# A decoder step on one core: each engine's instruction order taken from the scheduler's timeline simulation

## Chip, cores, metric

One core of one Trainium2 chip runs the whole program. The metric is device time in microseconds (us) of one launch, input and output transfers of the kernel's own queues included; lower is better.

## What is computed

One layer (DEPTH = 1) of a decoder for a prompt group of 1024 positions and a sample group of 8 sequences by 8 positions with 512 cached positions each. All in fp32; D_MODEL = 1024, D_FF = 2816.

```
xn = rmsnorm(x) ; z = xn @ w_in                     # 1024 -> 2820 columns, four head groups
y  = [ RG-LRU(z_A) | gated short conv(z_B) | forgetting attention(z_C) | differential attention(z_D) ]
x  = x + y @ w_out
x  = x + (silu(rmsnorm(x) @ w_gate) * (rmsnorm(x) @ w_up)) @ w_down
y_out = rmsnorm(x)                                  # plus the new K/V rows and states as outputs
rg_lru: r, i = sigmoid(...);  a = exp(-8 r softplus(-lam));  u = sqrt(1 - a*a) * i * x;  h = a*h + u
```

## The kernel before, in words

The weights come in fp32 and every product with them is made of three matmuls on split operands: a high part (`xTh`, `whi`) and the rest (`xTl`, `wlo`). `mm3` (L92) issues the three in a row: L94 high by high, L95 and L96 the two mixed ones. The split of a weight block is one ScalarE copy (L325) and one subtraction on VectorE or GpSimd (L326); blocks come from `WStream.load_to` (L310, L312) into a ring of three `raw` buffers on SyncE's queue.

The prompt is worked in two halves of 512 positions, the sample group beside the first. A list of small closures, `prog`, is the program's order: the norms and the input projection of half 0, then half 1; attention of half 0 mixed by cost (`merge`, L1252) into the projection of half 1; the output projection, mixed with the sample group's attention (L1421 transposes of cached keys, L1436 scores, L1509 values); attention of half 1 mixed into the first feed-forward blocks; then the feed-forward network, most of it as a seven-product Winograd form (L1743). `run` (L1270) calls the closures in order, which only traces instructions.

Attention is a chain for each pair of query blocks: scores on TensorE (L1057, L1061), maximum on VectorE (L1081 to L1097), exponential on ScalarE (L1099, and a scaling L1103), transposes on TensorE (L1141), their split on ScalarE and VectorE (L1145, L1146), values on TensorE (L1161), sum (L1173, L1178). The RG-LRU gates are two small matmuls for each chunk (L854) with sigmoids (L855), an exponential and a tanh (L860, L861) and a square root (L870) on ScalarE.

PSUM is eight banks: three `mm`, two `s`, two `t`, one `o`.

What the engines run is not the traced order. When the `with` block of the tile library's context closes, its scheduler plays the traced program through a simulated machine. Whenever an engine of that machine is free it gets an instruction whose inputs and buffers are ready there, the earliest in the traced order first; the order in which this happens is written out as that engine's order, which the chip then follows strictly. Only instructions passed through `keep` (`tc.keep_in_program_order`) stay in the traced order among each other. They are found in the head of the program (norm of the first half, its first projections) and at a few places behind it; nearly everything else is free.

## Time and profile before

| | |
|---|---|
| median of 3 runs | 1379.26 us (1373.75 to 1382.87) |
| the profiled execution | 1379.24 us, of which the span of its instructions is 1376.9 us |
| granted TensorE clock, mean | 0.991 |
| TensorE busy | 1345.7 us, 98% of the span |
| VectorE, ScalarE, GpSimd busy | 1060.9, 675.6, 126.7 us |

Busy time is the union of an engine's records. The granted clock is the share of 2.4 GHz that the throttle let through; 0.5 would be 1.2 GHz throughout. PEld is the weight load that goes before each matmul. A wait is idle time of an engine that ends when another engine, or a transfer, signals.

### The profile page before, as it was taken

The numbers are of one execution on the slowest core, as the hardware profiler recorded it, in microseconds if no ns is written. First come the engines' busy times: TensorE is split into PE (matmuls) and PEld (weight loads), VectorE is DVE, ScalarE is ACT, GpSimd is POOL, SyncE is SP. The second block draws the span as 40 slices with busy tenths as digits, with TensorE's granted clock in tenths as the row PEclk, the third lists the DMA queues.
The fourth block names the chain that finished last, engine by engine and source line by source line (L and its number), as shares of the span: only waits on it lengthen the run. The fifth ranks groups of instructions, "written<-read, shape, count | busy, mean of one in ns | idle before, by whom it ended". The sixth has DMA issues, their size and how long they took to land.

```text
span 1376.9 us, 23077 instructions
## 1 busy us (share of the span) xinstructions
PE 1345.7 (98%) x8477; PEld 1181.9 (86%) x8477; DVE 1060.9 (77%) x2699; ACT 675.6 (49%) x1326; POOL 126.7 (9%) x154
## 2 busy tenths in 40 slices
PE   9899998999999999999999999999999999999997
PEld 7799896878876688888888999997999999999996
DVE  6676377788556568899979988547998888888885
ACT  6575466756333258755544444324533444444454
POOL 3001012302243011000000000000200000000001
PEclk9999999999999999999999999999999999999999
DMA  8566438666994366444236433611624333333311
GB/s 260 175 194 205 132 125 266 205 201 222 343 333 142 108 216 217 139 138 123 77 115 196 125 92 93 191 47 62 197 63 123 93 92 92 93 92 93 93 47 69
DMA packets 202866, 202.65 MB, mean 147 GB/s; under 512 B 16529, under 2 KB 165549, under 8 KB 202626
## 3 DMA queue, kind: packets, MB, share of 16 engines
q1 hardware_dynamic: 189568, 168.60, 40.2%
q0 software_dynamic: 7328, 25.11, 5.0%
q10 hardware_dynamic: 5858, 7.47, 1.5%
q8 instruction: 67, 1.10, 0.3%
q14 instruction: 45, 0.37, 0.1%
HBM read 170.56 MB, written 32.29 MB: 147 GB/s over the span
## 4 chain that ended last, share of the span: by engine, by line
PE 81%; DVE 6%; ACT 6%; DMA 5%; issue 1%; SPq 0%; ACTq 0%; POOL 0%; DVEq 0%
PE pb_mm L94 11%; PE pb_mm L95 10%; PE pb_mm L96 10%; PE pb_mm L1743 8%; PE pb_s L1743 5%; PE pb_t L1743 5%; PE pb_t L94 3%; PE pb_t L95 2%; PE pb_t L96 2%; PE pb_o L1743 2%; PE pb_s L96 2%; PE pb_s L95 2%; PE pb_s L94 2%; PE pb_o L1161 2%; PE pb_t L1141 2%; DMA raw<-in_w_in_dram 2%
## 5 line engine op out<-in xcount | busy, mean ns | idle before, releaser
L325 ACT ACTIVATE whi<-raw 128x512 fp32r<-128x512 f32 (+1 forms) x409 | 251.8, 629 | 350.9 <-PE pb_mm L96 75.5
L326 DVE TENSOR_TENSOR wlo<-raw,whi 128x512 fp32r<-128x512 f32 (+1 forms) x405 | 275.8, 692 | 70.5 <-ACT whi L325 60.6
L94 PE MATMUL pb_mm<-xTh,whi 128*128 128x512 f32 (+2 forms) x536 | 192.3, 359 | 0.8 <-ACT whi L325 0.8
L95 PE MATMUL pb_mm<-xTl,whi 128*128 128x512 f32 (+2 forms) x536 | 191.1, 357 | 0.3 <-DVE xTl L452 0.3
L96 PE MATMUL pb_mm<-xTh,wlo 128*128 128x512 f32 (+2 forms) x536 | 190.6, 356 | 0.3 <-DVE wlo L326 0.3
L96 PEld LDWEIGHTS pb_mm<-xTh,wlo 128*128 128x128 f32 x536 | 101.0, 188 | 13.7 <-issue 1.6
L94 PEld LDWEIGHTS pb_mm<-xTh,whi 128*128 128x128 f32 x536 | 101.3, 189 | 12.7 <-ACT whi L325 1.1
L95 PEld LDWEIGHTS pb_mm<-xTl,whi 128*128 128x128 f32 x536 | 101.2, 189 | 10.8 <-DVE xTl L452 0.5
L94 PE MATMUL pb_mm<-whi,xTh 128*128 128x256 f32 (+1 forms) x312 | 91.1, 292 | 0.0
L1099 ACT ACTIVATE aP<-aP,anm 128x128 f32<-128x128 f32 (+7 forms) x96 | 74.0, 772 | 34.5 <-DVE anm L1097 32.2
L95 PE MATMUL pb_mm<-wlo,xTh 128*128 128x256 f32 (+1 forms) x312 | 88.3, 283 | 0.2 <-POOL wlo L326 0.2
L96 PE MATMUL pb_mm<-whi,xTl 128*128 128x256 f32 (+1 forms) x312 | 88.2, 283 | 0.0
L1829 DVE TENSOR_TENSOR acc<-acc,pb_mm 128x512 f32<-128x512 f32 (+1 forms) x95 | 64.4, 678 | 15.1 <-PE pb_mm L96 13.2
L94 PE MATMUL pb_mm<-whi,hTh 128*128 128x512 f32 (+1 forms) x179 | 70.7, 395 | 0.3 <-ACT hTh L1803 0.3
L96 PE MATMUL pb_mm<-whi,hTl 128*128 128x512 f32 (+1 forms) x179 | 70.6, 394 | 0.0
L95 PE MATMUL pb_mm<-wlo,hTh 128*128 128x512 f32 (+1 forms) x179 | 70.3, 393 | 0.0
L94 PEld LDWEIGHTS pb_mm<-whi,xTh 128*128 128x128 f32 x312 | 59.0, 189 | 5.0 <-issue 4.2
L95 PEld LDWEIGHTS pb_mm<-wlo,xTh 128*128 128x128 f32 x312 | 59.0, 189 | 0.8 <-POOL wlo L326 0.4
L96 PEld LDWEIGHTS pb_mm<-whi,xTl 128*128 128x128 f32 x312 | 58.9, 189 | 0.6 <-issue 0.4
L1743 PE MATMUL pb_mm<-xTh,whi 128*128 128x288 f32 (+1 forms) x184 | 53.7, 292 | 0.0
L1743 PE MATMUL pb_mm<-xTh,wlo 128*128 128x288 f32 (+1 forms) x184 | 53.6, 292 | 0.0
L1743 PE MATMUL pb_mm<-xTl,whi 128*128 128x288 f32 (+1 forms) x184 | 53.6, 292 | 0.0
(623 smaller groups left out, 3778.3 us busy)
## 6 DMA issues: line engine op xcount, KB each, us to landing
raw<-in_w_gate_dram SPq DMA_DIRECT2D x44, 512.0 KB
raw<-in_w_up_dram SPq DMA_DIRECT2D x44, 512.0 KB
raw<-in_w_down_dram SPq DMA_DIRECT2D x22, 1024.0 KB
raw<-in_w_in_dram SPq DMA_DIRECT2D x12, 1024.0 KB
raw<-in_w_in_dram SPq DMA_DIRECT2D x16, 512.0 KB
raw<-in_w_out_dram SPq DMA_DIRECT2D x8, 1024.0 KB
akt<-fkD SPq DMA_DIRECT2D x24, 256.0 KB
akt<-dkD SPq DMA_DIRECT2D x48, 128.0 KB
```

The lines of the kernel that those rows point to most:

```text
L94: kp(nc.tensor.matmul(out, lhsT=lh, rhs=rh, start=first, stop=False))
L95: kp(nc.tensor.matmul(out, lhsT=lh, rhs=rl, start=False, stop=False))
L96: kp(nc.tensor.matmul(out, lhsT=ll, rhs=rh, start=False, stop=last))
L325: i1 = nc.scalar.activation(hi, s, AF.Copy)
L326: i2 = (nc.gpsimd if pool else nc.vector).tensor_tensor(lo, s, hi.bitcast(F32), op=OP.subtract)
L1099: nc.scalar.activation(dst[:, :ln], dst[:, :ln], AF.Exp, bias=nmx, accum_out=sm)
L1141: nc.tensor.transpose(pt[:, o:o + 128], P[ti][:, kb * 128:(kb + 1) * 128], ident)
L1161: nc.tensor.matmul(po[:, q0:q0 + n], lhsT=v[:, kb, :], rhs=a[:, o:o + n], start=kb == 0 and i == 0, stop=kb >= nkb - 2 and i == 1, skip_gr ...
L1743: nc.tensor.matmul(pt, lhsT=w[:, k], rhs=x[:, k], start=first and k == 0 and i == 0, stop=k == 3 and i == 2, skip_group_check=True)
L1829: nc.vector.tensor_tensor(a, a, pt, op=OP.add)
```

## The change

One keyword is given to the tile library's context. With it the scheduler plays the program through the library's timeline simulation instead of its plain one; the traced program, the rule by which a free engine gets its next instruction, the pinned instructions, tiles and buffer counts stay the same. What can differ is the order on each engine and each queue, and with it the waits and the buffer that a tile gets.

```diff
-    with _tile.TileContext(nc) as tc:
+    with _tile.TileContext(nc, schedule_with_timeline_sim=True) as tc:
         hybrid_step(tc, I, C, O)
```

## Rows read from the trace of the kernel before

**Rows 1.** The page, part 1: busy time, share of the span, instructions.
```profile
PE 1345.7 (98%) x8477; PEld 1181.9 (86%) x8477; DVE 1060.9 (77%) x2699; ACT 675.6 (49%) x1326; POOL 126.7 (9%) x154
```
**Rows 2.** Windows by stage: busy time of each engine, clock, DMA share, GB/s.
```profile
0.00:200.00 200.00, 190.91 (x1270) 173.53 (x1271) 130.62 (x341) 119.52 (x221) 26.12 (x34) 0.99 0.57 178
200.00:350.00 150.00, 141.67 (x834) 119.89 (x833) 117.68 (x502) 94.28 (x229) 32.87 (x45) 0.99 0.71 232
350.00:500.00 150.00, 145.32 (x1051) 111.97 (x1051) 81.40 (x213) 46.13 (x91) 38.78 (x48) 0.95 0.65 218
500.00:575.00 75.00, 73.90 (x429) 61.75 (x428) 64.16 (x213) 59.93 (x108) 10.02 (x19) 1.00 0.67 213
575.00:700.00 125.00, 124.98 (x653) 103.49 (x652) 118.68 (x373) 73.24 (x138) 4.09 (x4) 1.00 0.36 107
700.00:975.00 275.00, 274.60 (x1729) 244.50 (x1728) 210.00 (x417) 113.05 (x211) 0.00 (x0) 1.00 0.40 121
975.00:1350.00 375.00, 375.00 (x2428) 350.82 (x2427) 323.13 (x603) 157.31 (x300) 10.05 (x3) 1.00 0.31 92
1350.00:1377.00 27.00, 19.35 (x96) 15.96 (x94) 15.23 (x43) 12.11 (x30) 4.80 (x2) 0.92 0.25 88
```
**Rows 3.** Windows of 25 us in which the granted clock is below 0.95.
```profile
50.00:75.00 25.00, 22.27 (x154) 20.94 (x154) 21.20 (x98) 12.64 (x28) 0.00 (x0) 0.93 0.64 192
275.00:300.00 25.00, 22.96 (x122) 18.50 (x120) 20.60 (x94) 14.53 (x39) 0.00 (x0) 0.93 0.59 175
425.00:450.00 25.00, 22.36 (x135) 14.63 (x135) 16.92 (x46) 7.78 (x15) 5.04 (x6) 0.81 0.26 88
450.00:475.00 25.00, 24.82 (x158) 15.50 (x154) 12.09 (x34) 5.88 (x12) 0.94 (x1) 0.91 0.33 106
```
**Rows 4.** Waits of PE: us in total, times, longest.
```profile
PE pb_t L967 <- DVE lgf L953: 3.1, 2, 2.7
PE pb_t L1141 <- ACT aP L1103: 2.2, 5, 0.6
PE pb_o L1161 <- DVE aAl L1146: 2.0, 1, 2.0
PE pb_s L1061 <- DMA akt<-dkD: 1.7, 1, 1.7
```
**Rows 5.** Timeline of PE around one of these waits (start, us, instruction).
```profile
281.07 0.40 PE L95 MATMUL pb_mm<-xTl,whi 128*128 128x512 f32 x1
283.14 0.33 PE L1061 MATMUL pb_s<-akt,aqt 128*128 128x128 f32 x1 [1.67 <-DMA akt<-dkD]
283.31 0.45 PE L96 MATMUL pb_mm<-xTh,wlo 128*128 128x512 f32 x1
```
**Rows 6.** Groups of ScalarE by line: table loads of the RG-LRU gates.
```profile
L855 ACT ACT_TABLE_LOAD x7 | 9.0, 1283 | 0.7 <-PE pb_t L854 0.5
L860 ACT ACT_TABLE_LOAD x4 | 5.1, 1283 | 0.1
L870 ACT ACT_TABLE_LOAD x4 | 5.1, 1283 | 0.1
```
**Rows 7.** Timeline of ScalarE around one table load.
```profile
83.20 0.19 ACT L430 ACTIVATION_READ_ACCUMULATOR nxs<-nxt 128x1 f32 x1
83.40 1.28 ACT L855 ACT_TABLE_LOAD   x1
84.70 0.89 ACT L855 ACTIVATE lr<-pb_t,colR 128x288 f32<-128x288 f32 x2
```
**Rows 8.** Waits of PEld for the gates' ScalarE work.
```profile
PEld pb_t L854 <- ACT lr L855: 1.0, 2, 0.7
```
**Rows 9.** Waits of SyncE's queue before weight loads.
```profile
SPq L310 <- DVE wlo L326: 172.5, 16, 17.4
SPq L312 <- DVE wlo L326: 137.8, 16, 16.8
```
**Rows 10.** The chain that ended last: its one long transfer after 575 us.
```profile
952.29 4.02 DMA raw<-in_w_gate_dram
```

## The prediction

> **What bounds the kernel now.** First the page's busy line [rows 1]: TensorE is busy in 1345.7 us of a span of 1376.9, so 31.2 us are all that any order can take from its idle time. The same instructions run after the change, in another sequence; TensorE's 8477 matmuls and their weight loads don't get fewer or shorter by being reordered. Then the windows by stage [rows 2], to see where the 31.2 us lie. The reader subtracts the first busy figure from the length of each stretch: 9.1 us in 0 to 200 (norms, projections, RG-LRU), 8.3 in 200 to 350 (attention of half 0), 4.7 in 350 to 500 (sample attention and output projection), 1.1 in 500 to 575 and 7.7 in the last 27 us; from 575 to 1350, more than half of the span, 0.4 us in 775. In that part no order can be better, only worse. Third, the granted clock, since a low clock makes TensorE busy for longer without idling [rows 3]: four windows of 25 us have 0.93, 0.93, 0.81 and 0.91. Time at the lower of the two levels (1.2 GHz) does half the work, so the loss in full-clock time is (0.07 + 0.07 + 0.19 + 0.09) x 25 = 10.5 us. Fourth, what ended TensorE's waits [rows 4]: single events of 0.5 to 3 us, each an instruction that stood first in TensorE's order while its input came late. The timeline at one of them shows what kind of thing it is [rows 5]: the source issues L94, L95 and L96 in a row, but the order has an attention score (L1061) between L95 and L96, and it waits 1.67 us for a key transfer while L96, which then runs within 0.2 us, was held behind it. So the scheduler does move instructions, and its simulated machine was wrong there about when the transfer lands. That is the one thing the change touches.
>
> **The change term by term**, against the profiled execution's own 1379.24 us (span 1376.9 and 2.3 around it; the median of the runs is 1379.26, and the runs spread over 9 us, so 1% is about what a measurement of this kernel can tell from no change).
>
> 1. *The work.* The same instructions, 0.
>
> 2. *Waits taken away.* A model that places inputs in time better would not put an instruction first whose input is late. The trace does not show the new order, so I bound it. Most: half of the idle time of 0 to 575 us, (9.1 + 8.3 + 4.7 + 1.1) / 2 = 11.6, and half of the clock's 10.5, 5.2; together 16.8. Least: 0. I take the two longest single waits of attention in the rows, 2.0 (L1161) and 1.7 (L1061) [rows 4], as gone: -3.7. I stay near the low end because the list is long and its entries short: the next of its kind, L1141, is 2.2 us in five pieces, and removing one usually shows the next instruction of the same chain as the late one.
>
> 3. *Waits added.* Every place where the new order puts an instruction earlier than its input is a new wait, and behind it on TensorE wait all the ready matmuls, as L96 does above. Least 0; most, the idle time of 0 to 575 once more, 23.2, and the clock's 10.5 once more, 33.7. I take three waits of the size of the key transfer's, 3 x 1.7 = +5.1, since such waits are of one kind with those that the present order has.
>
> 4. *Table loads on ScalarE.* ScalarE reloads its function table when its order goes from one kind of function to another: 7 + 4 + 4 = 15 loads of 1.283 us in the lines of the gates alone [rows 6], 19.2 us. Their number hangs on ScalarE's order. They cost TensorE little: its loader waits 1.0 us in two events for this work [rows 8], because projection matmuls fill the time and ScalarE is busy in 119.5 of the first 200 us [rows 2]. Bounds: -1.0 if the loads that show are gone, +19.2 if as many come on top and all stand in TensorE's way. I take 0, the nearer row being the 1.0. The Trainium skill, ScalarE: Activation LUTs, section "What ACT_TABLE_LOAD costs", gives 1283 ns for the load and about 1380 ns for a drain, some 2.66 us for each switch. The row has the load, and no drain with it: the instruction before ends at 83.39, the load runs from 83.40 to 84.68 and the next activation starts at 84.70 [rows 7]. By the page 15 further loads would be an estimated 40 us of ScalarE.
>
> 5. *VectorE from 575 to 700* is busy in 118.7 of 125 us [rows 2], with TensorE never idle. If its order splits weights ahead of emptying PSUM banks, TensorE has no bank to write. What covers this is the set of eight banks, and 6.3 us of slack in the stretch. I take 0; if the cover is gone the cost is at most the slack's size again, +6.3, as VectorE's work itself fits.
>
> 6. *The transfer queues.* SyncE's queue waits for its weight buffers, 172.5 us in 16 events at one line and 137.8 in 16 at the other, always for VectorE's split [rows 9]: loads are issued when a buffer falls free, and TensorE does not wait for them. Late in the program one such load stands on the chain that ended last, 4.0 us, with TensorE hardly idle [rows 10]. An attention load moved ahead of a weight load in this queue delays that by its own transfer only. 0, bounds -0.4 (the idle time of 575 to 1350) and +4.0. GpSimd's queue is busy in 126.7 us in all [rows 1]; 0.
>
> 7. *The end.* The last 27 us have 7.7 without a matmul: the final norm and the store after the last products. These depend on each other and can't be reordered: 0, +-1.
>
> Sum: 1379.24 - 3.7 + 5.1 = 1380.6 us. That is, no change that a measurement can tell.
>
> **The rivals.**
>
> *Better order pays (faster).* For it: idle time and low clock in the first 575 us are of the order's making, as the 1.67 us wait shows. Against: entries are short and a chain's next member waits too; and the largest loss, 0.81 at 425 to 450, is where the sample group's chain has few matmuls left to fill with (135 matmuls in 25 us, against 162 in the mean of 975 to 1350 [rows 2, 3]). With both halves of term 2: 1379.24 - 16.8 = 1362.4.
>
> *Attention stages starve TensorE (slower).* One mechanism: in 200 to 500, chains of attention and sample work are slotted between dense matmuls, and the new order puts them a little too early. Each event is 0.5 to 2 us, with the clock falling after a group of them, as in the windows of 275, 425 and 450. Price: the idle time of 200 to 575 a second time, 8.3 + 4.7 + 1.1 = 14.1, and the clock's loss there, (0.07 + 0.19 + 0.09) x 25 = 8.75, together 22.9: 1402. It decides once the added waits are over about 14 us, eight of the 1.7 us kind. For it: TensorE has no more than 1 to 2% idle to give, and every misjudged input costs directly. Against: waiting instructions need their inputs late on the chip, and the present order, also made on a model, keeps such events to some 14 us.
>
> *Table switches (slower).* ScalarE takes sigmoids, exponentials and square roots of the gates as they come ready, and doubles its 15 loads; TensorE's transposes and gate matmuls in 75 to 190 us wait for banks behind them: 1379.24 + 19.2 = 1398.4. It decides when TensorE waits for more than half of the new loads. Against it: the covering matmuls of this stretch, and ScalarE's 80 us of idle time in the first 200. The Trainium skill, ScalarE: Activation LUTs, section "Table sets: the hidden batching unit", has the rule beside it: batch activations by set, not by function. By that rule an order that follows readiness alone would pay here; the trace so far shows the loads and nearly no wait for them.
>
> *Nothing to see.* The two simulated machines agree wherever it matters, and what moves stays within slack: 1379.2.
>
> **How the numbers follow.** Forecast (mixed, within 1%) 0.45; nothing to see 0.06; better order pays 0.19; attention starves 0.20; table switches 0.10. Faster by over 1% (under 1365.5): 0.19. Within 1%: 0.51. Slower by over 1% (over 1393): 0.30. For the range I reach from just below the faster rival, 1360, to above the slower ones, 1406, which leaves out the outer parts of these three, some 0.2 in all; the bound of term 3, 1413, is in that rest. The forecast's own range is 1366 to 1393.
>
> **What would show it.** The number of instructions per engine stays (table loads apart). From 575 to 1350 the windows show TensorE idle under 2 us. The idle time of 0 to 575 stays between 15 and 35 us, with other lines among its enders. The loads of L855, L860 and L870 are 10 to 20. If a window after 575 has TensorE idle by several us, the reason is a bank or a weight buffer that VectorE's new order frees late, and terms 5 and 6 were wrong; if the clock falls in more windows than four, term 3 was too small; if idle time before 575 is below 12 us, term 2 was.

## The result and the profile after

The changed kernel takes 1445.66 us (median of four runs, 1444.07 to 1449.28) against 1377.99 us (four runs): a ratio of 1.050 with a 95% interval of 1.0475 to 1.0526. The forecast was no change, 1380.6, with a range up to 1406; it was wrong by 65 us.

The profiled execution took 1444.07 us with a span of 1442.3. The page's busy line (busy time, share of the span, instructions), which answers to [rows 1]:

```profile
PE 1372.7 (95%) x8477; PEld 1207.1 (84%) x8477; DVE 1067.7 (74%) x2699; ACT 674.1 (47%) x1326; POOL 121.4 (8%) x154
```

The counts are those of before. TensorE idles for 1442.3 - 1372.7 = 69.6 us, 38.4 more than before, and is busy for 27.0 us more with the same matmuls; 38.4 + 27.0 = 65.4 is the whole difference of the spans. The windows by stage, with the columns of [rows 2], say where:

```profile
0.00:200.00 200.00, 188.87 (x1235) 172.46 (x1236) 121.06 (x320) 116.48 (x219) 23.68 (x32) 0.97 0.56 176
200.00:350.00 150.00, 146.63 (x879) 128.28 (x877) 128.77 (x506) 95.23 (x233) 35.07 (x49) 1.00 0.75 246
350.00:500.00 150.00, 131.09 (x938) 97.67 (x936) 73.63 (x199) 39.74 (x79) 34.80 (x42) 0.92 0.56 186
500.00:575.00 75.00, 74.47 (x373) 60.96 (x374) 47.62 (x132) 36.52 (x66) 6.30 (x13) 1.00 0.53 163
575.00:700.00 125.00, 125.00 (x664) 106.23 (x663) 100.46 (x278) 74.00 (x132) 7.50 (x11) 1.00 0.49 146
700.00:975.00 275.00, 252.56 (x1572) 224.40 (x1572) 212.75 (x518) 115.95 (x218) 1.82 (x2) 0.93 0.37 112
975.00:1350.00 375.00, 371.76 (x2324) 341.86 (x2323) 316.11 (x612) 157.36 (x301) 7.54 (x3) 1.00 0.32 94
```

The idle time has gone down by 5.0 us in 200 to 350, the first half's attention, and up by 14.2 in 350 to 500 and by 22.0 in 700 to 975, a stretch that had 0.4 before. The windows of 25 us in which most is lost, with the granted clock in the third column from the end (answering to [rows 3]):

```profile
25.00:50.00 25.00, 21.27 (x156) 20.64 (x155) 10.16 (x28) 10.61 (x24) 7.73 (x12) 0.84 0.68 213
350.00:375.00 25.00, 18.27 (x112) 16.87 (x111) 10.10 (x35) 6.21 (x16) 3.84 (x4) 0.71 0.81 287
375.00:400.00 25.00, 21.06 (x134) 18.28 (x132) 7.47 (x15) 3.95 (x7) 9.10 (x11) 0.81 0.87 281
725.00:750.00 25.00, 25.00 (x124) 20.79 (x123) 23.45 (x58) 11.65 (x23) 0.00 (x0) 1.00 0.19 53
750.00:775.00 25.00, 18.78 (x81) 13.20 (x79) 21.59 (x93) 13.34 (x26) 1.82 (x2) 0.70 0.13 43
800.00:825.00 25.00, 17.75 (x89) 14.76 (x89) 19.53 (x45) 10.50 (x17) 0.00 (x0) 0.86 0.61 182
825.00:850.00 25.00, 20.97 (x119) 20.07 (x120) 17.74 (x35) 10.47 (x21) 0.00 (x0) 0.73 0.65 194
```

From 575 to 750 TensorE is full at 1.00, and in the next window it is not. What ran out there is seen when TensorE's matmuls are counted by line, those of the attention (L1057, L1061, L1141, L1161, L1205, L1221; 848 in all) and the dense ones (projections and feed-forward), as started by a time:

| us | before: dense / attention | after: dense / attention |
|---|---|---|
| 500 | 2251 / 264 | 2168 / 264 |
| 600 | 2479 / 589 | 2508 / 409 |
| 700 | 2780 / 814 | 2819 / 625 |
| 750 | 2977 / 848 | 2996 / 690 |
| 800 | 3277 / 848 | 3032 / 844 |

Before, the second attention ends near 713 us, with dense matmuls left for 56 us until the Winograd blocks begin (first L1743 at 769). After, TensorE is ahead with the dense work by 700 and at 750 has used it up, while 158 attention matmuls remain; in the next 50 us only 36 dense ones run. Then the Winograd blocks start without their weights prepared: of the 22.4 us that TensorE idles from 700 to 975, 11.1 lie in 750 to 800, beside the end of the attention, and 11.3 in 800 to 850, most of them in front of Winograd products (L1743). The one long piece of the chain that ended last in this stretch is a load of them (start, us), which answers to [rows 10]:

```profile
825.84 8.09 DMA raw<-in_w_up_dram
```

Why the attention falls behind is seen in TensorE's timeline. ScalarE has finished the first high part for the value products at 576.62 (the two L1145 together run from 576.02 to 577.11):

```profile
576.74 0.40 PE L95 MATMUL pb_mm<-wlo,hTh 128*128 128x512 f32 x1
576.98 0.39 PE L96 MATMUL pb_mm<-whi,hTl 128*128 128x512 f32 x1
...
579.77 0.39 PE L96 MATMUL pb_mm<-whi,hTl 128*128 128x512 f32 x1
580.00 0.28 PE L1161 MATMUL pb_o<-aAh,avt 128*128 128x256 f32 x1
```

Fourteen dense matmuls go ahead of the value product that was ready at 576.62. This is no wait, TensorE is busy throughout, and so no list of waits shows it. Over the 160 split parts that the value products read, 3.9 matmuls of other work start, in the mean, between the end of a split and the first product that reads it in the kernel before, and 11.9 in the changed one. Between the first score and the last value product of the second attention TensorE's order has 527 dense matmuls before, in runs of 3.5 in the mean (1 of 150 runs has nine or more), and 726 after, in runs of 8.1 (36 of 90).

The list of TensorE's waits, with the columns of [rows 4], has new entries, all short; the last three are of the stretch from 750 to 850:

```profile
PE pb_mm L94 <- ACT xTh L565: 6.2, 2, 3.7
PE pb_t L1141 <- DVE aP L1113: 4.0, 3, 2.3
PE pb_t L1421 <- DMA spgk<-in_cache_fox_k_dram,idx: 3.9, 1, 3.9
PE pb_t L1221 <- DVE arb L1216: 3.9, 2, 3.6
PE pb_s L1743 <- ACT whi L325: 3.1, 1, 3.1
PE pb_s L1061 <- DVE aP L1084: 2.3, 3, 1.4
PE pb_t L1743 <- DVE wtl L1669: 2.1, 2, 2.0
```

ScalarE's table loads by line, which answer to [rows 6], are the same; with the smaller groups there are 24 in either profile:

```profile
L855 ACT ACT_TABLE_LOAD x7 | 9.0, 1283 | 2.6 <-PE pb_t L854 2.5
L860 ACT ACT_TABLE_LOAD x4 | 5.1, 1283 | 0.1
L870 ACT ACT_TABLE_LOAD x4 | 5.1, 1283 | 0.1
```

And SyncE's queue stands twice as long before the weight loads of L310, and less before those of L312 [rows 9]:

```profile
SPq L310 <- DVE wlo L326: 349.2, 28, 18.9
SPq L312 <- DVE wlo L326: 109.5, 18, 17.7
```

### The profile page after: what moved, and what is told of

Same layout as the page of the kernel before. It is cut to its first block, busy times and chain, and to the rows that moved or that the text cites. A ratio compares the mean times of both kernels' runs of the same rounds, so it can differ in the third digit from the quotient of the medians.

```text
span 1442.3 us, 23079 instructions
## 1 busy us (share of the span) xinstructions
PE 1372.7 (95%) x8477; PEld 1207.1 (84%) x8477; DVE 1067.7 (74%) x2699; ACT 674.1 (47%) x1326; POOL 121.4 (8%) x154
## 4 chain that ended last, share of the span: by engine, by line
PE 85%; DVE 6%; DMA 4%; ACT 3%; issue 1%; SPq 1%; ACTq 0%; POOL 0%; DVEq 0%
PE pb_mm L94 12%; PE pb_mm L95 12%; PE pb_mm L96 12%; PE pb_mm L1743 7%; PE pb_t L1743 5%; PE pb_s L1743 5%; PE pb_t L94 3%; PE pb_t L95 3%; PE pb_t L96 3%; PE pb_o L1161 2%; PE pb_s L95 2%; PE pb_s L94 2%; PE pb_s L96 2%; PE pb_t L1141 2%; PE pb_o L1743 2%; PE pb_s L1057 1%
## 5 line engine op out<-in xcount | busy, mean ns | idle before, releaser
L325 ACT ACTIVATE whi<-raw 128x512 fp32r<-128x512 f32 (+1 forms) x409 | 248.9, 627 | 332.8 <-PE pb_mm L96 64.8
L326 DVE TENSOR_TENSOR wlo<-raw,whi 128x512 fp32r<-128x512 f32 (+1 forms) x405 | 279.0, 706 | 65.2 <-ACT whi L325 61.7
L95 PEld LDWEIGHTS pb_mm<-xTl,whi 128*128 128x128 f32 x536 | 100.9, 188 | 14.2 <-issue 1.3
L94 PE MATMUL pb_mm<-whi,xTh 128*128 128x256 f32 (+1 forms) x312 | 94.0, 303 | 9.4 <-ACT xTh L565 6.2
L95 PE MATMUL pb_mm<-wlo,xTh 128*128 128x256 f32 (+1 forms) x312 | 92.0, 297 | 0.0
L94 PEld LDWEIGHTS pb_mm<-whi,xTh 128*128 128x128 f32 x312 | 63.0, 202 | 14.0 <-ACT xTh L565 6.8
L95 PEld LDWEIGHTS pb_mm<-wlo,xTh 128*128 128x128 f32 x312 | 63.2, 203 | 1.3 <-issue 0.8
L1146 DVE TENSOR_TENSOR aAl<-pb_t,aAh 128x512 fp32r<-128x512 f32 (+1 forms) x80 | 50.1, 633 | 17.1 <-ACT aAh L1145 14.6
L1145 ACT ACTIVATE aAh<-pb_t 128x512 fp32r<-128x512 f32 (+1 forms) x80 | 42.7, 552 | 31.2 <-PE pb_t L1141 28.1
L1743 PE MATMUL pb_mm<-xTh,whi 128*128 128x288 f32 (+1 forms) x184 | 54.5, 296 | 1.5 <-DVE wv L1752 1.5
```

Source lines behind the costliest of these rows:

```text
L94: kp(nc.tensor.matmul(out, lhsT=lh, rhs=rh, start=first, stop=False))
L95: kp(nc.tensor.matmul(out, lhsT=lh, rhs=rl, start=False, stop=False))
L325: i1 = nc.scalar.activation(hi, s, AF.Copy)
L326: i2 = (nc.gpsimd if pool else nc.vector).tensor_tensor(lo, s, hi.bitcast(F32), op=OP.subtract)
L1145: nc.scalar.activation(ah[:, :o], pt[:, :o], AF.Copy)
L1146: nc.vector.tensor_tensor(al[:, :o], pt[:, :o], ah[:, :o].bitcast(F32), op=OP.subtract)
```

## The experiments

In E1 to E11 an engine is *held* to an order: after the program is traced, each instruction of the engine is made to come after the one ahead of it in a list that was read from one of the two compiled programs. The scheduler still orders the engines that are not held. In the traces of E5 and E6 each engine runs the same lines in the same sequence as the kernel whose order it is held to (in E6 one pair on ScalarE is swapped). The core of the edit, with the list left out (in E1 to E4 it stands at the top of the file, and line numbers in their traces are 22 higher):

```diff
+def impose(tc):
...
+    by = {i.name: i for i in tc.nc.cur_bb.bb.instructions}
+    info = mybir.DependencyInfo(mybir.DependencyClass.NoSync, mybir.DependencyReason.DATA)
...
+        for a, b in zip(keep, keep[1:]):
+            tc.add_manual_dep(by[b], a, info, reason="order")
...
         hybrid_step(tc, I, C, O)
+        impose(tc)
```

All times, with the ratio to the kernel before on the same chip:

| run | scheduler | held | us | ratio, 95% interval |
|---|---|---|---|---|
| E1 | timeline | TensorE as before | 1445.18 | 1.0467 (1.0411 to 1.0524) |
| E2 | plain | TensorE as after | 1448.39 | 1.0486 (1.043 to 1.0541) |
| E3 | timeline | TensorE, after then before | 1430.03 | 1.0354 (1.0306 to 1.0402) |
| E4 | timeline | TensorE, before then after | 1464.19 | 1.0597 (1.0545 to 1.0648) |
| E5 | timeline | all five as before | 1390.29 | 1.0051 (1.003 to 1.0073) |
| E6 | plain | all five as after | 1445.80 | 1.0444 (1.0407 to 1.0481) |
| E7 | timeline | TensorE, VectorE, ScalarE as before | 1395.01 | 1.0085 (1.0056 to 1.0114) |
| E8 | timeline | TensorE, VectorE as before | 1415.08 | 1.0223 (1.0198 to 1.0248) |
| E9 | timeline | TensorE, ScalarE as before | 1421.45 | 1.0273 (1.0246 to 1.03) |
| E10 | plain | all five, after then before | 1400.37 | 1.0134 (1.0109 to 1.0159) |
| E11 | plain | all five, before then after | 1435.15 | 1.0379 (1.0356 to 1.0403) |
| E12 | timeline | none; attention traced earlier | 1444.50 | 1.0474 (1.0452 to 1.0497) |
| E13 | timeline | none; P3B 18 | 1411.59 | 1.0245 (1.0228 to 1.0262) |
| E14 | plain | none; P3B 18 | 1385.12 | 1.0061 (1.0031 to 1.0091) |
| E15 | plain | none; attention traced earlier | 1393.03 | 1.0107 (1.0079 to 1.0134) |

**E1 and E2, TensorE's order alone.** My first theory, from the timeline above, was that TensorE's order holds the loss.

```diff
+_ORDER = {'PE': <order of the kernel before (E1), of the changed kernel (E2)>}
```

> The changed kernel, but TensorE alone is held to the order that it has in the kernel before; the scheduler's timeline simulation still orders the other four engines around that. Theory A (the loss is in TensorE's order: attention matmuls stand behind more dense ones, so the chain of the attention takes more dense work for each step and its last part runs uncovered): 1378 us, 1370 to 1388, and the mean time from the end of VectorE's split at L1146 to the next matmul of L1161 is back from 2.07 us to under 0.9. Theory B (the orders of VectorE, ScalarE and SyncE delay the chain): it stays near 1440, over 1425. If both have a part: between 1390 and 1425.

> The kernel before, but TensorE alone is held to the order that it has in the changed kernel; the plain scheduler orders the other four engines around that. Theory A (TensorE's order holds the loss): 1445 us, 1430 to 1455, with the same windows of low clock and the link from L1146 to L1161 near 2 us. Theory B (the orders of the other engines): 1378 to 1395.

E2 came out as theory A has it, E1 as theory B. In E1 the link that A is about is cured (1.31 us in the mean from a split part to its value product, 1.21 before, 3.31 after), and yet a loss of the same size is there: TensorE now waits, mostly for VectorE. It lies in other places, though: up to 500 us TensorE idles 50.0 us in E1 and 33.4 in the changed kernel; from 700 to 975 it is 9.5 against 22.4. Its waits in E1:

```profile
PE pb_t L1243 <- DVE arb L1238: 9.6, 4, 4.5
PE pb_mm L116 <- ACT xTh L587: 6.4, 2, 3.9
PE pb_mm L116 <- DVE acc L1630: 5.2, 1, 5.2
PE pb_t L116 <- DVE xTl L474: 4.9, 2, 3.1
```

So TensorE's order is enough to lose the time (E2), but a loss of this size comes about without it too (E1): theory A falls as the only cause.

**E3 and E4, TensorE's order by halves of the program.**

```diff
+_ORDER = {'PE': <one order up to the last L1509, the other from there>}
```

> The changed kernel, TensorE held to the changed kernel's order up to the last matmul of L1509 (the end of the sampling in the first half, near 500 us), and from there to the order of the kernel before. Theory A, with the two losses that the trace of after shows (about 21 us up to there, about 42 us from there to 860 us) independent of each other: 1378 + 21 = 1399 us, 1392 to 1408. If a late first part also spoils the second: above 1415. Theory B: near 1440.

> The changed kernel, TensorE held to the order of the kernel before up to the last matmul of L1509, and from there to the changed kernel's order. Theory A, with the two losses independent: 1378 + 42 = 1420 us, 1410 to 1430, with the windows of low clock between 750 and 850 us kept (20 us earlier) and those before 500 as in the kernel before. Theory B: near 1440.

Both missed, by 31 and 44 us. With only TensorE held, the other engines' orders are made anew around it, and E1 had shown that these lose time too. The two runs don't locate anything by themselves; for that all engines have to be held.

**E5, E6 and E7, all engines.** The two compiled programs differ in one more thing. In the traces the transfers of SyncE's and ScalarE's queues signal eight completion semaphores between them, and which transfers share one differs between the programs. In ScalarE's timeline of the changed kernel a store stands at its issue:

```profile
15.00 0.36 ACT L743 ACTIVATE vo<-pb_mm 128x256 f32<-128x256 f32 x1
20.38 0.35 ACTq L746 DMA_DIRECT2D out_p_fox_v_dram<-vo  x1
20.78 0.42 ACT L748 ACTIVATE vs<-vo 128x256 fp32r<-128x256 f32 x1 [5.42 <-DMA waT<-in_lru_w_a_dram]
21.11 0.58 ACT L565 ACTIVATE xTh<-pb_t 128x512 fp32r<-128x512 f32 x1
```

The store L746 could be issued at 15.36; it stands for 5 us, in a wait on the semaphore that it signals itself, until a load of another tile (`waT`) that signals the same one has landed. Behind it stands L565, for which TensorE waits. Before, the same instructions run in the same sequence, the store signals another semaphore than that load, and it is issued at once:

```profile
15.40 0.35 ACTq L746 DMA_DIRECT2D out_p_fox_v_dram<-vo  x1
```

That gave theory D.

```diff
+_ORDER = {'PE': ..., 'DVE': ..., 'Activation': ..., 'SP': ..., 'Pool': ...}   # E5 before, E6 after
+_ORDER = {'PE': ..., 'DVE': ..., 'Activation': ...}                           # E7 before
```

> The timeline simulation is still on, but all five engines are held to the order of the kernel before. What is left of the change is which of the eight completion semaphores each transfer is given, and with it the transfers behind which the issue of another must wait. Theory C (the orders of several engines carry the loss, each alone enough to lose it all): 1378 us, 1370 to 1388. Theory D (the loss is in the semaphores: an issue on ScalarE's or SyncE's queue stands until an earlier transfer with the same semaphore has landed, and everything behind it on that engine stands too, as in the changed kernel at 15 to 20 and 24 to 32 us, where ScalarE stood 5.0 and 7.9 us before L746): over 1420. Both: between.

> The reverse: the plain scheduler, all five engines held to the order of the changed kernel; only the semaphores of the transfers are given out as the plain scheduler does. Theory C (orders): 1445 us, 1432 to 1455. Theory D (semaphores): under 1400.

> The timeline simulation on, TensorE, VectorE and ScalarE held to the order of the kernel before; SyncE, GpSimd and the semaphores are free. Theory C with the loss in the three compute engines: 1380 us, 1372 to 1392. If SyncE's order of loads carries a part: 1395 to 1430, and e5 is then faster than this by that part. Theory D: as e5, over 1420.

The orders hold the loss: with all five held, the plain scheduler loses 61.7 us (E6) and the timeline one 6.2 (E5, 2 us over the range of theory C, on a chip on which the kernel before takes 1384.1). With the orders equal, the semaphores are the one difference that the traces show, so the 6.2 us are put down to them; the buffers that tiles get, which the traces don't tell apart, were not tested. In E5 the store is still late:

```profile
15.01 0.36 ACT L743 ACTIVATE vo<-pb_mm 128x256 f32<-128x256 f32 x1
19.58 0.37 ACTq L746 DMA_DIRECT2D out_p_fox_v_dram<-vo  x1
```

Matmul by matmul, E5 is 8.8 us behind the kernel before at 50 us and 12.2 at 400, and falls no further behind from there. E7 is 4.7 us above E5, with intervals that overlap: no cost of SyncE's and GpSimd's own orders is shown once the three compute engines are held.

**E8 and E9, which engine beside TensorE.**

```diff
+_ORDER = {'PE': ..., 'DVE': ...}          # E8, before
+_ORDER = {'PE': ..., 'Activation': ...}   # E9, before
```

> The timeline simulation on, TensorE and VectorE held to the order of the kernel before; ScalarE, SyncE, GpSimd and the semaphores are free. Theory C1 (beside TensorE's order it is VectorE's that loses the time, since with TensorE alone held most of TensorE's waits end on VectorE): 1390 to 1400 us, as with three engines held. Theory C2 (it is ScalarE's): over 1425. Both needed: 1405 to 1425.

> The timeline simulation on, TensorE and ScalarE held to the order of the kernel before; VectorE, SyncE, GpSimd and the semaphores are free. Theory C1 (VectorE's order carries the second half of the matter): 1435 to 1450 us. Theory C2 (ScalarE's): 1390 to 1405.

Neither alone: E8 loses 31.5 and E9 37.8 us, against 64.8 in E1 and 10.9 in E7. E8 is in the range given for both being needed, and E9 lies between its two ranges. Holding VectorE beside TensorE gives back 33 us, holding ScalarE 27, both together 54. The two gains nearly add up, so either engine's order carries a part.

**E10 and E11, where in the program.** All five engines held, the two orders joined at the end of the first half's sampling.

```diff
+_ORDER = {'PE': <after up to there, before from there>, 'DVE': ...}   # E10, five engines
+_ORDER = {'PE': <before up to there, after from there>, 'DVE': ...}   # E11, five engines
```

> The plain scheduler, all five engines held to the order of the changed kernel up to the last matmul of L1509 (the end of the sampling in the first half) and from there to the order of the kernel before. With the losses of the two parts independent, as the traces have them: 1378 + 21 = 1399 us less the part of the head that the semaphores hold (about 7), so 1392, 1387 to 1405. If a late first part also spoils the second: over 1415.

> The plain scheduler, all five engines held to the order of the kernel before up to the last matmul of L1509 and from there to the order of the changed kernel. With the losses independent: 1378 + 42 = 1420 us, 1412 to 1435, with TensorE's clock under 0.9 in the 100 us behind the end of the second attention. If the second part's order only fits a late first part: above 1440.

The losses are nearly independent: 16.7 and 51.5 us, 68.2 together, against 61.7 in E6. E10 lost 3 us more than the 14 expected, since the head is late in it without the semaphores too, by VectorE's order (E6 and E10 have it alike; VectorE's timeline of E6, then TensorE's three longest waits in E10):

```profile
34.31 0.22 DVE L275 TENSOR_TENSOR raw<-raw 128x64 f32<-128x64 f32 x1 [11.52 <-DMA raw<-in_diff_lambda_dram]
34.57 0.22 DVE L276 TENSOR_REDUCE raw<-raw 128x2 f32<-128x64 f32 x1
34.71 1.28 DVE L566 TENSOR_TENSOR xTl<-pb_t,xTh 128x512 fp32r<-128x512 f32 x2
```

```profile
PE pb_mm L96 <- DVE xTl L566: 9.5, 1, 9.5
PE pb_mm L96 <- DMA xTl<-yD: 3.2, 1, 3.2
PE pb_t L1421 <- DMA spgk<-in_cache_fox_k_dram,idx: 2.8, 1, 2.8
```

A small product of constants stands ahead of the activations' split L566 and waits 11.5 us for its transfer. E11 lost 9 us more than the 42 expected. It has the second loss alone; its windows of 500 to 700 and 700 to 900, with the latter of the kernel before as the third line:

```profile
500.00:700.00 200.00, 200.00 (x1029) 168.54 (x1028) 149.30 (x413) 113.30 (x201) 13.85 (x24) 1.00 0.51 156
700.00:900.00 200.00, 178.23 (x981) 153.68 (x981) 165.78 (x416) 88.86 (x168) 1.82 (x2) 0.87 0.33 99
700.00:900.00 200.00, 199.93 (x1288) 180.68 (x1287) 160.23 (x302) 83.00 (x153) 0.00 (x0) 1.00 0.45 137
```

**E12 and E15, an earlier place in the program.** In the code the attention's place among the dense work is set by two fractions.

```diff
-P2_FRAC = 0.8
+P2_FRAC = 0.6
-P3_FRAC = .75
+P3_FRAC = 0.55
```

> The changed kernel with both attentions traced earlier among their dense work: P2_FRAC 0.6 in place of 0.8 and P3_FRAC 0.55 in place of 0.75, so that the attention's last step is traced with 40 and 45% of the dense work behind it. Theory E (under the timeline simulation the place of a step in the program no longer sets its place on TensorE; the number of dense matmuls that go ahead of a ready attention matmul does): no change, 1437 to 1453 us, and the last matmul of L1161 in the second half starts within 10 us of the changed kernel's 796. The rival (the attention is merely traced too late for this scheduler, and a lead mends it): 1385 to 1425.

> The kernel before with P2_FRAC 0.6 and P3_FRAC 0.55, the lead that left the changed kernel's time and TensorE's attention alone. Theory E: under the plain scheduler the lead moves the attention: the last L1161 of the second half starts 15 to 45 us earlier than in the kernel before (704), and the time moves by -5 to +25 us. The rival (the lead has no effect under either): 704 within 5, and 1378 within 5.

Theory E held in both. The first and last starts of the high-part value products (first E12, then E15; durations are min/median/max in ns):

```profile
L1161 PE MATMUL pb_o<-aAh,avt x160: 218/281/582, 236.5 to 798.6; 128*128 128x256 f32 x128, 128*128 128x128 f32 x32
```

```profile
L1161 PE MATMUL pb_o<-aAh,avt x160: 218/281/392, 219.8 to 681.0; 128*128 128x256 f32 x128, 128*128 128x128 f32 x32
```

Under the timeline simulation the lead changes neither the time nor the end of the attention: other instructions do trade places, but the last L1161 of these starts at 798.6 (796.4 in the changed kernel) and stands at the same place of TensorE's order, 4498th. Under the plain one it comes at 681.0 in place of 704.1, and the kernel is 1.1% slower (two runs).

**E13 and E14, more cover.** Six blocks more of the feed-forward network are put beside the second attention.

```diff
-P3B = 12
+P3B = 18
```

> The changed kernel with P3B 18 in place of 12: six more blocks of gate and up projections in the dense work that runs beside the second attention, taken from the work behind it (and done without the half-block products, so with somewhat more work in all; the next run has the same change under the plain scheduler and is the measure). Theory F (the second part loses because its cover runs out): with six blocks more the program's order ends the attention before the cover ends, TensorE stays at 25 of 25 us in every window from 550 to 900, and the time is 20 to 35 us above the next run's in place of 65. The rival (each late step costs time, covered or not): 55 to 75 above it.

> The kernel before with P3B 18 in place of 12: the same six blocks moved and done without the half-block products. By both theories only the added work counts here, since the attention was covered already: six blocks times 1/8 of about 11 us, so 5 to 10 us above the kernel before, 1383 to 1392.

With the edit the changed kernel takes 1411.6 us, 26.5 above its counterpart E14 in place of 65 to 68: theory F. Its attention is slower still in time (it ends at 844 us), but the Winograd blocks begin only at 884, and TensorE never idles beside it; windows of E13:

```profile
750.00:775.00 25.00, 25.00 (x127) 20.97 (x126) 23.12 (x75) 10.80 (x20) 0.00 (x0) 1.00 0.17 46
775.00:800.00 25.00, 25.00 (x133) 21.06 (x131) 21.49 (x56) 14.58 (x28) 1.85 (x2) 1.00 0.33 105
825.00:850.00 25.00, 25.00 (x119) 20.56 (x118) 18.11 (x42) 7.66 (x13) 0.00 (x0) 1.00 0.19 64
```

What is left, 26.5, is of the size of E10's and E5's losses together (16.7 + 6.2), and it lies where theirs do: up to 500 us TensorE idles 32.4 us in E13, 33.4 in the changed kernel and 22.1 before. No version beats the kernel before.

## Why the prediction was wrong

*What bounds the kernel: the step that failed.* The windows were read rightly, but from "0.4 us of idle time in 775" I took that little could happen from 575 to 1350, and priced terms 5 and 6 there with at most +6.3 and +4.0. A stretch without idle time tells that it is covered, not by how much. The reserve could have been read: the second attention ended at 713 and the next blocks began at 769, 56 us of dense work after an attention of 211 us (from its first score at 502). An attention slower by more than a quarter runs out of cover. It took 272 us (532 to 804); E11 measures 51.5 us for this part, and E13 shows that the cover is the cause, since with more of it TensorE does not idle there at all. Of the signs that the prediction named, TensorE's idle time from 575 to 1350 is the one that came out otherwise: 25.7 us, not under 2.

*Term 1* held: the same counts.

*Term 2* was right in kind. TensorE idles 3.4 us in place of 8.3 in the first half's attention, a gain of 5.0 against the 3.7 taken, but in that stretch 612 dense matmuls ran in place of 542, and behind it, from 350 to 500, 456 in place of 574. That the gain was paid for with the dense work missing there is read from these counts, not tested by a run.

*Term 3* was mis-sized for the first part: terms 2 and 3 together were put at +1.4, and E10 measures +16.7, inside the term's bound of 33.7. The longest waits there are few, as assumed, but 9.5, 3.2 and 2.8 us long in place of 1.7. And its mechanism, an instruction placed too early which then waits, is only a part of it: the other part is a ready instruction placed too late, which no list of waits shows. As the text said, the clock then fell in more windows than four.

*Term 4* held: 24 table loads in either profile, and the rival that counted on more of them is out. The rule in the Trainium skill, ScalarE: Activation LUTs, section "Table sets: the hidden batching unit", is to batch activation calls by set, not by function; this order needed no more loads than the old one, so no run here shows what breaking up sets costs.

*Term 5* named a bank or weight buffer that VectorE frees late as what a loss after 575 would mean. From 575 to 700 nothing of the kind is seen: VectorE is less busy there than before (100.5 us against 118.7) and TensorE does not idle. Behind 750 some waits are of this kind (scores that wait for VectorE to read their bank, 2.3 us at L1084; Winograd products that wait for VectorE's split, 2.1 at L1669), but they come when the dense work that covered such waits has run out.

*Term 6*: E7 against E5 shows no cost of SyncE's own order beyond 5 us, and that is within the noise. What I had not thought of is the semaphores of the transfers, 6.2 us in E5.

*Term 7*: TensorE idles 10.0 us in the last 27; before it was 7.7. Little of the difference is there.

*The rivals.* "Attention stages starve TensorE" had the right kind of stage and the wrong size: 22.9 us, since its price was the idle time that the old order has, a second time, and only from 200 to 575. Starvation is not bounded by what the old order shows. The part behind the first half's sampling (from near 500 us), where the old order hardly starved, holds three quarters of the loss.

What stays open is why the timeline simulation lets so many dense matmuls go ahead of a ready attention step; E12 shows that tracing the attention earlier does not change it. How the 51.5 us of E11 divide between the three engines' orders is open too, since E1 and E2 show losses of the same size with TensorE's order as before and as after.

## What to carry to other kernels

Where a stretch is full because one kind of work covers a chain of another, ask for the reserve: how much covering work is left when the chain ends, and by how many per cent the chain may slow down before it runs out. When an order changes, look beside the waits at how long ready instructions stand behind others on a busy engine, by counting matmuls by kind over time. And to test an order, hold all engines to it: with one held, the others are ordered anew around it and the result does not locate the loss.

## What was not expected of the hardware

In the changed kernel a store on ScalarE's queue that shares its completion semaphore with an unfinished load held ScalarE for 5.0 us at its issue, and the next one, near 32 us, for 7.9; with the orders equal, what is left of the change costs 0.5% (E5). And most of the added 27.0 us of busy time goes with the clock: summed over the whole windows of 25 us, (1 - granted clock) x 25 is 11.8 us before and 37.8 after, idle time in these windows included. The low windows are those where TensorE idles or has just idled, down to 0.70 at 750 to 775, straight behind a window of 1.00. Not every window with idle time is low: 450 to 475 has 4.9 us of it at 1.00.
